# The order of the matmuls within a 128-row chunk of the weight-stationary products

## The chip, the cores and the metric

The kernel runs on one core of one Trainium2 chip. The metric is the device time of one execution in microseconds (us); the median over repeated runs counts. Inputs and outputs are float32 in device memory.

## What is computed

One layer of a decoder trunk on 256 tokens of width 2048, then a final norm. Cut to what matters:

```
h = rms_norm(x);  z = h @ w_in                                  # 2048 x 5144
x = x + concat[gating(z), dilated_attention(z), nsa(z)] @ w_out   # 2048 x 2048
h = rms_norm(x);  m = rms_norm(mem)
x = x + cross_attention(h @ wq, m @ wkv) @ wo
h = rms_norm(x)
x = x + square(relu(h @ w_up)) @ w_down                         # 2048 x 8192, 8192 x 2048
return rms_norm(x)
```

Nearly all of the arithmetic is in the products with weight matrices, and most of that in `w_up` and `w_down`.

## The kernel before

**Products in three parts.** A float32 operand is split into two float32r parts, hi and lo = x - hi. A product sums hi\*hi + hi\*lo + lo\*hi in PSUM. For weights, `split_w` makes `wh` on ScalarE (line 82) and then `wl` on VectorE (line 83) from a loaded block `raw` of 128 x 1024 numbers; `wh` and `wl` have three buffers each, `raw` five. For activations the hi and lo parts of a 128-feature chunk lie side by side, so that one matmul can stream both: 256 tokens of hi, then 256 tokens of lo, 512 columns.

**Two ways round.** `gemm` (line 193) holds activations stationary and streams 512 columns of weights; `w_down` goes that way (tile `dn`, line 207, three matmuls of 512 columns for a chunk). `gemm_t` (line 174) holds weights stationary and streams activations. It makes 256 output features at a time, as two halves f = 0 and f = 1 of 128; each half has one PSUM bank of 512 columns in the tile `acc`, and `acc` has two buffers. `w_up` (tile `up`), `w_out` (`wo`), the queries (`cq`, `bq`, `xq`), keys (`k`, `bk`, `mk`), the gating input (`u`) and the inputs of the compressed branch (`cmp`, issued by a loop of its own at line 259) go that way.

**The function at issue.** `products_t` (line 154) adds one weight block, four chunks kk of 128 rows, to an `acc`. For each chunk and each half it issues two matmuls:

- the **main** one (line 161): 128 weight columns of `wh`, 512 columns of activations (hi and lo), into the whole bank;
- the **low** one (line 165): 128 weight columns of `wl`, 256 columns of activations (hi alone), into the first half of the same bank.

Each matmul has a weight load of its own (LDWEIGHTS, listed as engine PEld). The order within a chunk is low f0, main f0, low f1, main f1, so 256- and 512-column matmuls alternate. Only in the first chunk of an `acc` does main come ahead of low in each half, since the first matmul into a bank must write all of it. After 16 chunks (64 matmuls) `join` (line 185) reads the bank with ScalarE and VectorE.

**The order of the program.** The text of the kernel is not the order on an engine: a scheduler places the instructions of all engines by its own model of their costs, so matmuls of neighbouring tiles can be mixed, and the lists under "The change" show what it made of each version. Weight blocks arrive by DMA issued from SyncE's queue.

**How many.** `products_t` issues 1024 pairs of main and low for `up` (4 quarters of 8 tiles of 32 pairs), 256 for `wo`, 128 for `cq`, and 64 each for `cmp`, `k`, `bk`, `bq`, `u`, `mk` and `xq`: 1856 in all.

Of the kernel before, what the change touches and what calls it, by code (L numbers as in the profile page):

```python
# [13 lines left out]
PSUM = bass.MemoryType.PSUM  # L14

P = 128
S = 256
# [13 lines left out]
# column blocks of w_in that come out transposed, two 128-wide features a pair  # L31
CMP, UU, KV, CQ, BK, BQ = 0, 2, 4, 6, 10, 12
# the parts that a product in float32r takes: hi*hi, hi*lo, lo*hi
# [4 lines left out]
def trunk_kernel(ctx: ExitStack, tc: tile.TileContext, a, out):  # L38
    """Every product with a weight matrix takes its float32 operands as two float32r parts, hi and
    lo = x - hi (exact), and sums hi*hi + hi*lo + lo*hi in PSUM.  # L40

    Activations that feed a product lie transposed, [features, part, tokens], both parts side by side.
    A product comes out transposed (weights stationary, in two halves: hi*hi + lo*hi and hi*lo) or
    with tokens on partitions (activations stationary)."""
    nc = tc.nc
# [12 lines left out]
    ones = cp.tile([P, P], F32, name="ones")  # L58
    nc.vector.memset(ones, 1.0)
    # brings the activation table in before the first data  # L60
# [13 lines left out]
    loads = []  # L74
# [10 lines left out]
    def split_scaled(hi, lo, src, g):  # L85
        """hi + lo = src * g, with g one number a partition."""
        nc.scalar.activation(hi, src, AF.Copy, scale=g)
        nc.vector.scalar_tensor_tensor(lo, src, g, f32(hi), op0=ALU.mult, op1=ALU.subtract)

    def put_act(tiles, k0, src, gi):  # L90
        """src [P, n, S], features k0 .. k0 + n, times their gains."""
        for i in range(src.shape[1]):
            k = k0 + i
            t = tiles[k // 4]
            split_scaled(t[:, k % 4, 0, :], t[:, k % 4, 1, :], src[:, i, :], gT[:, gi, k:k + 1])

# [1 line left out]
    def add_squares(ssq, src, first, eng=None):  # L98
        """ssq [P, 2, S] += src ** 2."""
        sq = ssq if first else sp.tile([P, 2, S], F32, tag="sq", name="sq")  # L100
        if eng is None:
            nc.scalar.activation(sq, src, AF.Square)  # L102
        else:
            eng.tensor_tensor(sq, src, src, op=ALU.mult)
        if not first:
            nc.gpsimd.tensor_tensor(ssq, ssq, sq, op=ALU.add)  # L106

    def mean_eps(ssq, name):
        """mean over features of the squares, + eps: [P tokens, 2]."""
        s = cp.tile([P, 2], F32, name=name)  # L110
        ps = pmisc.tile([P, 2], F32, tag="sc", name="pss")
        nc.gpsimd.tensor_tensor(ssq[:, 0, :], ssq[:, 0, :], ssq[:, 1, :], op=ALU.add)
        for t in range(2):
            nc.tensor.matmul(ps[:, t:t + 1], ssq[:, 0, t * P:(t + 1) * P], ones[:, 0:1], start=True, stop=True)
        nc.vector.tensor_scalar(s, ps, 1.0 / D, EPS, op0=ALU.mult, op1=ALU.add)
        return s
# [6 lines left out]
    def along_free(r, name):  # L123
        """r [P tokens, 2] as [P, S], the same on every partition."""
        b = cp.tile([P, S], F32, name=name)
        ps = pmisc.tile([P, S], F32, tag="sc", name="psb")
        for t in range(2):
            dg = sp.tile([P, P], F32, tag="dg", name="dg")
            nc.vector.tensor_scalar_mul(dg, ident, r[:, t:t + 1])
            nc.tensor.matmul(ps[:, t * P:(t + 1) * P], ones, dg, start=True, stop=True)  # L130
        nc.scalar.activation(b, ps, AF.Copy)
        return b

# [8 lines left out]
    def gemm_t1(x, wsrc, name):  # L142
        """Like gemm_t for a contraction of 512, with one sum: [P, 2 features, tokens]."""
        acc = pacc.tile([P, 2, 2, S], F32, tag="acc", name=name)
        wh, wl = (w.rearrange("p (k n) -> p k n", k=4) for w in split_w(load_raw(wsrc)))
        for kk in range(4):
            for f in range(2):
                fs = slice(f * P, (f + 1) * P)
                for j, (w, l) in enumerate(((wh, 0), (wh, 1), (wl, 0))):
                    nc.tensor.matmul(acc[:, f, 0, :], w[:, kk, fs], x[:, kk, l, :],  # L150
                                     start=(kk == 0 and j == 0), stop=(kk == 3 and j == 2))
        return acc

    def products_t(acc, x, wh, wl, first, last):
        """acc [P, 2 features, hi*hi + lo*hi | hi*lo, tokens] += four 128-row chunks of the contraction."""
        for kk in range(4):
            for f in range(2):
                fs = slice(f * P, (f + 1) * P)

                def main(start, stop):  # L160
                    nc.tensor.matmul(acc[:, f].rearrange("p a s -> p (a s)"), wh[:, kk, fs],  # L161
                                     x[:, kk].rearrange("p a s -> p (a s)"), start=start, stop=stop)

                def low():
                    nc.tensor.matmul(acc[:, f, 0, :], wl[:, kk, fs], x[:, kk, 0, :], start=False, stop=False)  # L165

                if first and kk == 0:
                    main(True, False)
                    low()
                else:  # L170
                    low()
                    main(False, last and kk == 3)

    def gemm_t(lhs, wsrc, name, order=None, between=None):
        """Two 128-wide features, transposed: [P, 2 features, hi*hi + lo*hi | hi*lo, tokens]."""
        acc = pacc.tile([P, 2, 2, S], F32, tag="acc", name=name)
        order = order or list(range(len(lhs)))
        for n, b in enumerate(order):
            wh, wl = (w.rearrange("p (k n) -> p k n", k=4) for w in split_w(load_raw(wsrc[b])))
            products_t(acc, lhs[b], wh, wl, n == 0, n == len(order) - 1)  # L180
            if between is not None:
                next(between, None)
        return acc

    def join(acc, name, dst=None):
        """The two halves of gemm_t, added."""
        lo = sp.tile([P, 2, S], F32, tag="half", bufs=3, name="half")
        nc.scalar.activation(lo, acc[:, :, 1, :], AF.Copy)  # L188
        d = lo if dst is None else dst
        nc.vector.tensor_tensor(d, acc[:, :, 0, :], lo, op=ALU.add)  # L190
        return d

    def gemm(lhs, wsrc, kb, n, name, between=None, hold=0):
        """Tokens on partitions: [P, 2, n]; blocks of kb 128-row chunks of the contraction. The last
        hold blocks stay, and the first tokens go through all of them before the others."""
# [67 lines left out]
    def consts(them):  # L263
        """Not ahead of the weights asked for so far."""
# [16 lines left out]
    # nothing is scaled before the norm is there  # L281
# [24 lines left out]
    # lo, hi and none: one product with hi and one with lo sum what is needed in two halves  # L306
# [6 lines left out]
    def compress():  # L313
        for m, which in enumerate(("k", "v")):
# [7 lines left out]
            # rows 0..29: hi*hi + hi*lo, rows 30..59: lo*hi  # L322
# [26 lines left out]
            else:  # L349
                # v_c of a group at the partitions 32 h of each of its heads  # L350
# [24 lines left out]
    # no compressed block lies before the first rows  # L375
# [8 lines left out]
    def softmax_pair(sc0, sc1, m0, m1, name):  # L384
        """Masked scores of two heads (or branches), both token tiles: exp(s - max) and its sums."""
# [15 lines left out]
    def scale_and_transpose(v0, v1, r, name):  # L401
        """p * r, transposed: [keys, 2, 384], the first 256 columns of keys 0..127, then 128 of the rest."""
# [20 lines left out]
    mix = [None] * 4  # L423
    for g in range(2):
# [5 lines left out]
        # compressed branch, four heads at once  # L430
# [135 lines left out]
    # w_out: the spatial gating's features last; the memory's loads among the products  # L566
# [76 lines left out]
    for q in range(4):  # L643
# [16 lines left out]
        for n in range(4):  # L660
# [3 lines left out]
            for t in range(2):  # L664
# [7 lines left out]
                if q == 3 and n == 2:  # L672
                    # what the last quarter adds comes to this
# [43 lines left out]
def _blocks(w, kb, n):  # L717
    """[K, N] -> [N / n, K / (128 kb), 128, kb * n]: what one partition reads is contiguous."""
    k = w.shape[0]
# [3 lines left out]
def _arrays(np, i):  # L723
# [15 lines left out]
    # cmp, u, selected k, window k, NSA q, dilated k, dilated q  # L739
# [43 lines left out]
```

## Time and profile before

| | |
|---|---|
| median of 3 runs | 1216.53 us (1216.46 to 1218.69) |
| profiled execution, from its first to its last instruction | 1216.0 us |
| TensorE matmuls (PE) busy | 1187.0 us, 98% |
| TensorE weight loads (PEld) busy | 1021.3 us, 84% |
| VectorE (DVE) busy | 750.9 us, 62% |
| ScalarE (ACT) busy | 588.3 us, 48% |
| DMA, mean over the span | 184 GB/s |
| granted TensorE clock, mean | 0.993 |

The profile lists no separate device time for the profiled execution; its span stands 0.5 us under the median of the runs. An engine's busy time is the union of its instructions' spans. Matmuls overlap: the next one starts before the one ahead of it has left the array, so what a matmul costs is the distance between the starts of two matmuls, not its listed length. The listed ends of matmuls are modelled; the starts are recorded.

### The profile page before, as it was taken

What the parts mean: (1) busy time and instruction counts of PE and PEld (TensorE: products, weight loads), DVE (VectorE), ACT (ScalarE), POOL (GpSimd) and SP (SyncE); (2) the same over time, 40 slices, a digit from 0 to 9 for tenths busy, and PEclk for the clock granted to TensorE, in tenths of its full rate; (3) what the DMA queues carried; (4) which work ended last, traced back from release to release, by engine and by line L of the source; (5) the groups of instructions that cost most, each with busy time, mean ns of one, the idle gap of its engine ahead of it and who ended that gap; (6) DMA issues with size and microseconds to landing.
All of it is one profiled execution on the core that took longest, in us unless ns stands there. A gap on an engine that the chain in (4) does not pass through costs nothing.

```text
span 1216.0 us, 16456 instructions
## 1 busy us (share of the span) xinstructions
PE 1187.0 (98%) x6450; PEld 1021.3 (84%) x6450; DVE 750.9 (62%) x904; ACT 588.3 (48%) x800; POOL 61.3 (5%) x54
## 2 busy tenths in 40 slices
PE   5999999999999999999999999999999999999996
PEld 4899888888878888988888888888888888888885
DVE  8775788467687565865554556554565555566554
ACT  5464555365565455644433444433444433444443
POOL 7000000000033100200000000000000000000000
PEclk9999999999999999999999999999999999999999
DMA  6676533555657555555666655666556566655663
GB/s 228 196 252 209 157 122 122 182 158 172 190 191 224 176 172 174 181 177 192 189 195 191 191 186 182 192 201 193 187 178 192 191 196 195 186 185 185 195 189 104
DMA packets 65385, 224.24 MB, mean 184 GB/s; under 512 B 7963, under 2 KB 9499, under 8 KB 65179
## 3 DMA queue, kind: packets, MB, share of 16 engines
q1 hardware_dynamic: 65307, 223.19, 57.8%
q8 instruction: 50, 0.82, 0.3%
q14 instruction: 28, 0.23, 0.1%
HBM read 221.06 MB, written 2.10 MB: 184 GB/s over the span
## 4 chain that ended last, share of the span: by engine, by line
PE 91%; DVE 4%; issue 2%; ACT 1%; DMA 1%; SPq 0%; ACTq 0%; POOLq 0%; POOL 0%; DVEq 0%
PE dn L207 27%; PE up L161 20%; PE up L165 10%; PE wo L161 3%; PE cq L161 2%; DVE wl L83 2%; PE xo L150 2%; PE bv L207 2%; PE v L207 2%; PE mv L207 2%; PE wo L165 2%; PE cq L165 1%; PE xq L161 1%; PE mk L161 1%; PE u L161 1%
## 5 line engine op out<-in xcount | busy, mean ns | idle before, releaser
L83 DVE TENSOR_TENSOR wl<-raw,wh 128x1024 fp32r<-128x1024 f32 (+3 forms) x414 | 505.2, 1224 | 350.5 <-ACT wh L82 348.8
L82 ACT ACTIVATE wh<-raw 128x1024 fp32r<-128x1024 f32 (+3 forms) x414 | 428.8, 1038 | 459.9 <-PE dn L207 185.5
L161 PE MATMUL up<-h,wh 128*128 128x512 f32 x1024 | 359.3, 398 | 0.0
L207 PE MATMUL dn<-wh,hid 128*128 128x512 f32 x992 | 306.2, 389 | 0.0
L165 PE MATMUL up<-h,wl 128*128 128x256 f32 x1024 | 282.4, 281 | 0.0
L161 PEld LDWEIGHTS up<-h,wh 128*128 128x128 f32 x1024 | 190.6, 188 | 44.1
L207 PEld LDWEIGHTS dn<-wh,hid 128*128 128x128 f32 x992 | 186.2, 188 | 38.4
L165 PEld LDWEIGHTS up<-h,wl 128*128 128x128 f32 x1024 | 193.3, 189 | 2.7
L207 PE MATMUL dn<-wl,hid 128*128 128x512 f32 x496 | 193.1, 389 | 0.6 <-DVE sf L675 0.6
L207 PEld LDWEIGHTS dn<-wl,hid 128*128 128x128 f32 x496 | 93.1, 188 | 20.5 <-DVE wl L83 1.0
L161 PE MATMUL wo<-mix,wh 128*128 128x512 f32 x256 | 89.5, 395 | 0.4 <-ACT wh L82 0.4
L165 PE MATMUL wo<-mix,wl 128*128 128x256 f32 x256 | 70.7, 282 | 3.3 <-DVE wl L83 3.3
L161 PEld LDWEIGHTS wo<-mix,wh 128*128 128x128 f32 x256 | 47.5, 188 | 10.9 <-ACT wh L82 0.7
L165 PEld LDWEIGHTS wo<-mix,wl 128*128 128x128 f32 x256 | 48.3, 189 | 5.2 <-DVE wl L83 4.5
L188 ACT ACTIVATE half<-up 128x512 f32<-128x512 f32 x32 | 19.1, 597 | 56.7 <-PE up L161 56.7
L161 PE MATMUL cq<-hx,wh 128*128 128x512 f32 x128 | 45.5, 397 | 0.0
L190 DVE TENSOR_TENSOR half<-up,half 128x512 f32<-128x512 f32 x32 | 22.1, 692 | 35.5 <-ACT half L188 35.5
L106 POOL TENSOR_TENSOR ssq<-ssq,sq 128x512 f32<-128x512 f32 x21 | 30.6, 1456 | 174.6 <-ACT sq L102 174.2
L680 POOL TENSOR_TENSOR rf<-sf,mhalf 128x1 f32<-128x1 f32 x2 | 1.1, 560 | 706.8 <-DVE sf L678 706.8
L165 PE MATMUL cq<-hx,wl 128*128 128x256 f32 x128 | 35.3, 281 | 0.0
L161 PE MATMUL cmp<-hx,wh 128*128 128x512 f32 x64 | 27.6, 463 | 4.6 <-ACT wh L82 4.6
L666 DVE SCALAR_TENSOR_TENSOR xt<-dn,m,xt 128x512 f32<-128x512 f32 x32 | 22.6, 747 | 14.3 <-PE dn L207 14.3
(282 smaller groups left out, 1409.9 us busy)
## 6 DMA issues: line engine op xcount, KB each, us to landing
raw<-in_w_up SPq DMA_DIRECT2D x128, 512.0 KB, 4.3
raw<-in_w_down SPq DMA_DIRECT2D x128, 512.0 KB, 4.3
raw<-in_w_t SPq DMA_DIRECT2D x52, 512.0 KB, 3.6
raw<-in_w_out SPq DMA_DIRECT2D x32, 512.0 KB, 4.3
raw<-in_w_bv SPq DMA_DIRECT2D x8, 512.0 KB, 3.7
raw<-in_w_v SPq DMA_DIRECT2D x8, 512.0 KB, 3.5
raw<-in_w_mk SPq DMA_DIRECT2D x8, 512.0 KB, 4.2
raw<-in_w_q SPq DMA_DIRECT2D x8, 512.0 KB, 3.8
```

What stands on the lines that cost most here:

```text
L82: nc.scalar.activation(hi, src, AF.Copy)
L83: nc.vector.tensor_tensor(lo, src, f32(hi), op=ALU.subtract)
L106: nc.gpsimd.tensor_tensor(ssq, ssq, sq, op=ALU.add)
L150: nc.tensor.matmul(acc[:, f, 0, :], w[:, kk, fs], x[:, kk, l, :], start=(kk == 0 and j == 0), stop=(kk == 3 and j == 2))
L161: nc.tensor.matmul(acc[:, f].rearrange("p a s -> p (a s)"), wh[:, kk, fs], x[:, kk].rearrange("p a s -> p (a s)"), start=start, stop=stop)
L165: nc.tensor.matmul(acc[:, f, 0, :], wl[:, kk, fs], x[:, kk, 0, :], start=False, stop=False)
L188: nc.scalar.activation(lo, acc[:, :, 1, :], AF.Copy)
L190: nc.vector.tensor_tensor(d, acc[:, :, 0, :], lo, op=ALU.add)
L207: nc.tensor.matmul(acc[t][:, :n], lhs[k // 4][:, k % 4, l, ts], w[:, kk, :], start=(k == 0 and j == 0), stop=(k == KD - 1 and j == 2))
L666: nc.vector.scalar_tensor_tensor(xs, acc[t], r3[:, t:t + 1], xs, op0=ALU.mult, op1=ALU.add)
L680: nc.gpsimd.tensor_tensor(rf, s_, mhalf[:, 0:1], op=ALU.pow)
```

## The change

`products_t` issues a chunk's matmuls by kind rather than by half: both mains, then both lows. In the last chunk of an `acc` both lows come first, then both mains, so that the main still closes each bank. Nothing is added or removed; comments and docstrings fall away, and lines after the function move by two (line 165 becomes 166).

```diff
         for kk in range(4):
-            for f in range(2):
-                fs = slice(f * P, (f + 1) * P)
-
-                def main(start, stop):
-                    nc.tensor.matmul(acc[:, f].rearrange("p a s -> p (a s)"), wh[:, kk, fs],
-                                     x[:, kk].rearrange("p a s -> p (a s)"), start=start, stop=stop)
-
-                def low():
-                    nc.tensor.matmul(acc[:, f, 0, :], wl[:, kk, fs], x[:, kk, 0, :], start=False, stop=False)
-
-                if first and kk == 0:
-                    main(True, False)
-                    low()
-                else:
-                    low()
-                    main(False, last and kk == 3)
+            xk = x[:, kk].rearrange("p a s -> p (a s)")
+
+            def mains(start, stop):
+                for f in range(2):
+                    nc.tensor.matmul(acc[:, f].rearrange("p a s -> p (a s)"), wh[:, kk, f * P:(f + 1) * P], xk,
+                                     start=start, stop=stop)
+
+            def lows():
+                for f in range(2):
+                    nc.tensor.matmul(acc[:, f, 0, :], wl[:, kk, f * P:(f + 1) * P], x[:, kk, 0, :],
+                                     start=False, stop=False)
+
+            if last and kk == 3:
+                lows()
+                mains(False, True)
+            else:
+                mains(first and kk == 0, False)
+                lows()
```

**In the MLP's first product.** TensorE's list where one `up` tile ends and the next begins, before (the number behind a tile's name is a buffer's):

```order
L161 MATMUL up_8865<-h_4433,wh 128x512
L165 MATMUL up_8865<-h_4433,wl 128x256
L161 MATMUL up_8865<-h_4433,wh 128x512
L161 MATMUL up_8960<-h_4430,wh 128x512
L165 MATMUL up_8960<-h_4430,wl 128x256
L161 MATMUL up_8960<-h_4430,wh 128x512
L165 MATMUL up_8960<-h_4430,wl 128x256 x2
L161 MATMUL up_8960<-h_4430,wh 128x512
L165 MATMUL up_8960<-h_4430,wl 128x256
L161 MATMUL up_8960<-h_4430,wh 128x512
```

And the same place now:

```order
L166 MATMUL up_4862<-h_4433,wl 128x256 x2
L161 MATMUL up_4862<-h_4433,wh 128x512 x2
L166 MATMUL up_4862<-h_4433,wl 128x256 x4
L161 MATMUL up_4862<-h_4433,wh 128x512 x2
L161 MATMUL up_4963<-h_4430,wh 128x512 x2
L166 MATMUL up_4963<-h_4430,wl 128x256 x2
L161 MATMUL up_4963<-h_4430,wh 128x512 x2
L166 MATMUL up_4963<-h_4430,wl 128x256 x2
```

Before, two mains stood next to each other only where the tile changed, and two lows only where the new tile's first chunk ends; now they stand in twos throughout, and four lows and four mains meet at the tile's end.

**Where the program starts.** TensorE's list where the `cmp` products go over to the second block of x (`hx_81`), before:

```order
L165 MATMUL cmp_85<-hx_80,wl 128x256
L161 MATMUL cmp_85<-hx_80,wh 128x512
L165 MATMUL cmp_84<-hx_81,wl 128x256
L161 MATMUL cmp_84<-hx_81,wh 128x512
L165 MATMUL cmp_84<-hx_81,wl 128x256
```

And now:

```order
L161 MATMUL cmp_85<-hx_80,wh 128x512 x2
L166 MATMUL cmp_85<-hx_80,wl 128x256 x2
L161 MATMUL cmp_84<-hx_81,wh 128x512 x2
L166 MATMUL cmp_84<-hx_81,wl 128x256 x2
L161 MATMUL cmp_84<-hx_81,wh 128x512 x2
```

The first matmul of a new block was one that needs `wl`; it is now one that needs `wh`, and two mains stand ahead of the first that needs `wl`.

## Rows read from the trace of the kernel before

**Rows 1.** The page: span, and busy time, share and instructions of two engines

```profile
span 1216.0 us, 16456 instructions
...
PE 1187.0 (98%) x6450; PEld 1021.3 (84%) x6450; DVE 750.9 (62%) x904; ACT 588.3 (48%) x800; POOL 61.3 (5%) x54
```

**Rows 2.** Waits of PE: total us, times, longest us

```profile
PE cmp L165 <- DVE wl L83: 9.7, 4, 3.9
...
PE wo L165 <- DVE wl L83: 3.3, 3, 1.7
```

**Rows 3.** Chain that ended last, in order of time: start us, us, what

```profile
93.77 8.16 PE wv L207 x68
...
587.04 87.04 PE dn L207 x384
...
764.37 87.04 PE dn L207 x384
...
941.70 87.04 PE dn L207 x384
...
1119.04 57.13 PE dn L207 x252
```

**Rows 4.** Timeline of PE over a tile's end: start us, us, instruction, count

```profile
700.00 0.28 PE L165 MATMUL up<-h,wl 128*128 128x256 f32 x1
...
707.18 0.40 PE L161 MATMUL up<-h,wh 128*128 128x512 f32 x1
707.42 0.28 PE L165 MATMUL up<-h,wl 128*128 128x256 f32 x1
707.54 0.62 PE L161 MATMUL up<-h,wh 128*128 128x512 f32 x2
708.00 0.28 PE L165 MATMUL up<-h,wl 128*128 128x256 f32 x1
708.11 0.40 PE L161 MATMUL up<-h,wh 128*128 128x512 f32 x1
708.35 0.40 PE L165 MATMUL up<-h,wl 128*128 128x256 f32 x2
708.58 0.40 PE L161 MATMUL up<-h,wh 128*128 128x512 f32 x1
708.82 0.28 PE L165 MATMUL up<-h,wl 128*128 128x256 f32 x1
```

**Rows 5.** Timeline of PEld, the weight loads, in the same stretch

```profile
707.06 0.19 PEld L161 LDWEIGHTS up<-h,wh 128*128 128x128 f32 x1
707.18 0.19 PEld L165 LDWEIGHTS up<-h,wl 128*128 128x128 f32 x1
```

**Rows 6.** Timeline of PE in the same alternation in `wo`

```profile
371.03 0.39 PE L161 MATMUL wo<-mix,wh 128*128 128x512 f32 x1
...
374.50 0.39 PE L161 MATMUL wo<-mix,wh 128*128 128x512 f32 x1
```

**Rows 7.** The page: costliest groups, of the mains of `up`

```profile
L161 PE MATMUL up<-h,wh 128*128 128x512 f32 x1024 | 359.3, 398 | 0.0
```

**Rows 8.** Timeline of PE: the longest wait in `cmp`, the last in `wo`

```profile
30.43 0.58 PE L165 MATMUL cmp<-hx,wl 128*128 128x256 f32 x1 [3.92 <-DVE wl L83]
...
366.98 0.39 PE L165 MATMUL wo<-mix,wl 128*128 128x256 f32 x1 [1.75 <-DVE wl L83]
```

**Rows 9.** Stretches: us, then PE, PEld, DVE, ACT, POOL busy, PEclk, DMA share, GB/s

```profile
20.00:30.00 10.00, 4.62 (x16) 3.67 (x16) 10.00 (x8) 3.60 (x6) 9.06 (x7) 0.78 0.45 123
30.00:36.00 6.00, 5.57 (x18) 4.80 (x19) 4.24 (x7) 0.04 (x1) 0.00 (x0) 0.51 0.64 193
...
320.00:370.00 50.00, 46.34 (x260) 39.35 (x259) 41.13 (x49) 30.67 (x49) 12.94 (x9) 1.00 0.60 195
```

## The prediction

> **What bounds the kernel now.** Read the busy shares first: PE has 98% of the span, no other engine over 62% [rows 1]. So what counts is the spacing of matmuls, and the few places where PE waits. Read the waits next: the large ones are 9.7 us in `cmp` and 3.3 us in `wo`, all of lows (line 165) for `wl`, the last thing that VectorE makes of a block [rows 2]. Everywhere else the time is the sum of distances from one matmul's start to the next.
>
> The chain of work gives clean distances. In `dn` 384 matmuls of 512 columns take 87.04 us, 0.2267 us each; in `wv` 68 of 256 columns take 8.16 us, 0.1200 us each [rows 3]. A main and a low by themselves would thus cost 0.3467 us. In `up`, where they alternate, 21 pairs go from a low's start at 700.00 to one at 707.42: 0.3533 us a pair [rows 4]. Whole stages say the same: `dn` ends at 587.04 + 87.04 = 674.08 and begins again at 764.37, so the 256 pairs of a quarter of `up` took 90.29 us, 0.3527 us each (the next quarters 90.29 and 90.30) [rows 3]. So alternation costs 0.006 us a pair over the two kinds by themselves, 6.1 us over `up`'s 1024 pairs [rows 7]. That is what this change can move.
>
> Where the 0.006 us sits is seen in the weight loads. The load for a matmul starts when the matmul ahead of it starts: the load for a low starts at 707.18, with the main [rows 4, 5]. A load is listed with 0.19 us. Under a main (0.23 us) it is done in time; under a low (0.12 us) it isn't, and the main that follows is stretched: a main behind a low takes 0.24 us (707.18 to 707.42), while two mains together take 0.46 (707.54 to 708.00), so that one of them takes 0.22 to 0.23 [rows 4].
>
> **The change part by part.** *Dense stretches.* Every chunk becomes main, main, low, low; the lists show it everywhere but at tile ends, where four of a kind meet. One stretched main in a chunk instead of two. The trace of before holds both pieces: main, main 0.46 us; low, low 0.23 us (708.35 to 708.58) [rows 4]. Starts are rounded to 0.01, so a chunk is 0.69 to 0.70 us, where alternation has 2 x 0.3527 = 0.7054. I take 0.70, the upper end, since these pieces stood singly among alternating ones: 0.0054 us saved on a chunk, times 512 chunks of `up`, 2.8 us. The lower bound of a chunk is 2 x 0.3467 = 0.6934, all of the excess gone: 512 x 0.012 = 6.1 us.
>
> *The other products.* Leaving `cmp` aside there are 768 pairs, 384 chunks. Their alternation isn't always dear: in `wo` ten pairs go from 371.03 to 374.50, 0.347 us each, with no excess at all [rows 6]. So alternation has a dear and a free rhythm, and these stages have both. I take half of `up`'s saving: 0.0027 us. Of the chunks I leave out the 55 or so between 326 and 367 us (41 us less 3.3 of waits, at 0.70 each), where VectorE's 41.13 us of 50 [rows 9] and the wait at 366.98 [rows 8] say that `wl` sets the pace: 329 x 0.0027 = 0.9 us. Bounds: nothing, to 329 x 0.0066 (from 0.70 to the floor of 0.6934) = 2.2 us; below nothing where the free rhythm is lost (the third rival).
>
> *Waits for wl.* A block now begins with two mains, which need `wh` but not `wl`. Where PE waits for `wl`, 0.46 us of work moves ahead of the wait. In `cmp` the last wait is 3.92 us long and ends at 30.43 [rows 8]; VectorE was busy for all of the ten us before [rows 9], so PE's pace doesn't set when `wl` comes, and the three waits ahead of it give nothing that lasts. I count one such gain, 0.46 us, and another for the last wait in `wo`. Together 0.9 us; the bounds are zero (if hi and lo of the activations aren't there either) and 0.46 for each of the seven waits in these two [rows 2], 3.2 us. After the wait at 30.43 the granted clock is 0.51, the lower level of 1.2 GHz, in the stretch to 36 us [rows 9]: PE had been idle for 3.92 us before. With 0.46 us of work put in front of it the idle time is still some 3.5 us; I leave that stretch as it is.
>
> *What is not changed.* The matmuls, loads, DMAs and their order on SyncE's and GpSimd's queues are the same. On ScalarE and VectorE a few instructions of the attention stages change places; PE is not waiting there, and I price that at zero, within 1 us either way. `wh` is released by the second main and `wl` by the last low, 0.23 us apart at most, and no split was waited for in `up`. No wait is added: at a tile's end the mains still close both banks, and the next tile has the other buffer of `acc`.
>
> Sum: 2.8 + 0.9 + 0.9 = 4.6 us off a span of 1216.0, so 1211.4. The median of the runs lies 0.5 us over the span: **1211.9 us**.
>
> A rule to weigh against this. The measured distances depend on the neighbour: 0.24 us for a main behind a low against 0.2267 in a run of mains [rows 3, 4]. The Trainium skill, TensorE: Matmul & The Clock Gate, section Back-to-back issue gap, gives a matmul of N columns N/2.4 + 2.5 ns on its own, which knows no neighbour: 0.216 and 0.109 us here, the same sum in any order, no change from the dense stretches. The trace doesn't agree with its size (0.2267 and 0.1200) nor with its independence.
>
> **The rivals.**
>
> *No change in the dense stretches.* The 0.006 us may belong to each load that lies under a low, not to each main behind a low. In both orders half of the loads lie under lows, so a chunk would stay at 0.7054 and the second low would pay what the second main saves. For it: a low lasts 0.12 us, less than a load's listed 0.19. Against: in `wv` every load lies under a 256-column matmul and the spacing is a clean 0.1200 [rows 3]; low, low in `up` took 0.23 [rows 4]. Only the waits remain: 1216.5 - 0.9 = 1215.6 us.
>
> *All of the excess goes.* The stretch is a rhythm that a run of equal matmuls ends (`dn`, `wv`, and the free rhythm in `wo`). Then 6.1 + 2.2 + 0.9 = 9.2 us: 1207.3 us. Against: the pieces in [rows 4] still show 0.24 for a main behind two lows (708.58 to 708.82).
>
> *Slower.* Two lows in a row have two loads under them, one after the other, and the delay of the second adds to that of the first; both mains then are stretched to 0.24 and 0.235, as mains behind a low are now, and the lows keep their 0.118 each: 0.711 a chunk. That is 0.0056 us over alternation, on the same 512 + 329 chunks 4.7 us, less 0.9 for the waits: 1216.5 + 3.8 = 1220.3 us. It decides from the point at which a chunk costs over 0.7065 us, where the waits no longer pay for it. For it: the main behind two lows is no shorter than the one behind a single low. Against: the second main of [rows 4] is.
>
> That the change doesn't do what it says is ruled out by the lists: mains stand in twos throughout.
>
> **How the numbers follow.** A measurement of this kernel can tell about 0.2%, 2.4 us, from no change. Forecast (1209.5 to 1214.1): 0.55. No change: 0.21. All of it: 0.12. Slower: 0.12. Faster by over 0.2% takes the forecast and the full gain, 0.67, less a little that falls short: 0.66. Within 0.2% 0.22, slower 0.12. The range leaves out most of the slower case and the lower part of the full gain: 1207.0 to 1217.5.
>
> **What would show it.** In the chain, `up`'s quarter goes from 90.29 to about 89.6 us (128 chunks of 0.70); 88.8 is the full gain, 90.3 none, 91.0 the slower rival. In the timeline, main, main should read 0.46 and low, low 0.23 to 0.24 all along, with the second main at 0.22 to 0.23. The waits for `wl` in `cmp` and `wo` should each be some 0.4 us shorter. Quarters that stay at 90.3 make the prediction wrong; so does a second low that takes 0.13 us or more.

## The result and the profile after

The changed kernel takes 1211.3 us (median of 4 runs, 1208.45 to 1211.99) against 1217.23 us in the same comparison: ratio 0.9938, 95% interval 0.9923 to 0.9954, so 5.6 to 9.4 us less. It was forecast at 1211.9 us, with 4.6 us off the span; the span of the profiled execution fell by 6.8 us, from 1216.0 [rows 1] to 1209.2. That execution's own time was 1211.03 us, so 1.8 us lie around the span, not the 0.5 us that the prediction took from the median: two errors that partly cancel in the forecast time. The 0.5 us set the span of one execution against the median of others; every execution on record that lists both has 1.7 to 1.9 us around its span, those of the kernel before too.

The page of the changed kernel, its span and busy engines:

```profile
span 1209.2 us, 16465 instructions
...
PE 1184.4 (98%) x6450; PEld 1018.7 (84%) x6450; DVE 752.0 (62%) x904; ACT 585.7 (48%) x800; POOL 63.5 (5%) x54
```

TensorE is the bound as before [rows 1]. Its waits (total us, times, longest) answer to [rows 2]:

```profile
PE cmp L166 <- DVE wl L83: 7.9, 6, 4.0
PE cmp L161 <- ACT wh L82: 5.0, 3, 4.4
...
PE wo L166 <- DVE wl L83: 0.6, 1, 0.6
```

The waits for `wl` in `wo` have nearly gone, 0.6 us for 3.3; in `cmp` they are 7.9 for 9.7. The longest wait in `cmp` has neither become shorter nor ended earlier than in [rows 8], where it ended at 30.43 us:

```profile
30.45 0.80 PE L166 MATMUL cmp<-hx,wl 128*128 128x256 f32 x2 [4.04 <-DVE wl L83]
```

The chain that ended last, which answers to [rows 3]:

```profile
582.45 87.05 PE dn L209 x384
...
758.81 87.05 PE dn L209 x384
...
935.18 87.05 PE dn L209 x384
...
1111.54 57.15 PE dn L209 x252
```

A quarter of `up`, from the end of `dn` to its next start, is 758.81 - 582.45 - 87.05 = 89.31 us, then 89.32 and 89.31; it was 90.29. `dn` is as it was. The timeline of TensorE in `up` answers to [rows 4] (x2 stands for two in a row):

```profile
703.28 0.40 PE L166 MATMUL up<-h,wl 128*128 128x256 f32 x2
703.51 0.63 PE L161 MATMUL up<-h,wh 128*128 128x512 f32 x2
703.98 0.40 PE L166 MATMUL up<-h,wl 128*128 128x256 f32 x2
704.22 0.63 PE L161 MATMUL up<-h,wh 128*128 128x512 f32 x2
704.68 0.40 PE L166 MATMUL up<-h,wl 128*128 128x256 f32 x2
704.91 0.63 PE L161 MATMUL up<-h,wh 128*128 128x512 f32 x2
705.38 0.39 PE L166 MATMUL up<-h,wl 128*128 128x256 f32 x2
```

Two lows take 0.23 to 0.24 us and two mains 0.46 to 0.47; from 703.28 to 705.38 three chunks take 2.10 us, 0.70 each.

Where the 6.8 us went, by the first matmul of each stage in the two traces:

| stretch | before, us | after, us | difference |
|---|---|---|---|
| start to the first matmul of `k` (`cmp`) | 44.49 | 44.07 | -0.42 |
| `k` to `u` (attention, gating) | 253.32 | 252.97 | -0.35 |
| `wo` | 95.15 | 91.37 | -3.78 |
| `mk` to `xo` (cross attention) | 102.13 | 102.51 | +0.38 |
| `up`, first quarter | 91.79 | 91.36 | -0.43 |
| `up`, other three | 270.88 | 267.95 | -2.93 |
| `dn`, first three quarters | 261.12 | 261.15 | +0.03 |
| last `dn` and the tail | 97.16 | 97.86 | +0.70 |

So `up` gave 3.4 us, a little more than the 2.8 forecast, and `wo` 3.8, far more than the 1 us or less expected there. The tail gave 0.7 us back: the chain there goes through waits for splits and for DMA. This is not the price of arriving earlier, since groups of eight (below) arrive there earlier still and take 97.17 us for it, the 97.16 of before.

### The profile page after: what moved, and what is told of

It reads as the page before. It is cut to its first block, busy times and chain, and to the rows that moved or that the text cites. A ratio compares the mean times of both kernels' runs of the same rounds, so it can differ in the third digit from the quotient of the medians.

```text
span 1209.2 us, 16465 instructions
## 1 busy us (share of the span) xinstructions
PE 1184.4 (98%) x6450; PEld 1018.7 (84%) x6450; DVE 752.0 (62%) x904; ACT 585.7 (48%) x800; POOL 63.5 (5%) x54
## 4 chain that ended last, share of the span: by engine, by line
PE 91%; DVE 2%; DMA 2%; ACT 1%; issue 1%; ACTq 0%; POOLq 0%; POOL 0%; DVEq 0%
PE dn L209 27%; PE up L161 20%; PE up L166 10%; PE wo L161 4%; PE cq L161 2%; PE xo L150 2%; PE wo L166 2%; PE v L209 2%; PE bv L209 2%; PE mv L209 2%; PE k L161 1%; PE mk L161 1%; PE cq L166 1%; PE bq L161 1%; PE xq L161 1%; PE u L161 1%
## 5 line engine op out<-in xcount | busy, mean ns | idle before, releaser
L161 PE MATMUL up<-h,wh 128*128 128x512 f32 x1024 | 317.2, 395 | 0.0
L166 PEld LDWEIGHTS up<-h,wl 128*128 128x128 f32 x1024 | 187.6, 188 | 42.2
L166 PE MATMUL up<-h,wl 128*128 128x256 f32 x1024 | 197.0, 279 | 0.0
L161 PEld LDWEIGHTS up<-h,wh 128*128 128x128 f32 x1024 | 158.3, 189 | 2.6
L161 PE MATMUL wo<-mix,wh 128*128 128x512 f32 x256 | 79.6, 396 | 0.1
L166 PE MATMUL wo<-mix,wl 128*128 128x256 f32 x256 | 49.7, 280 | 0.6 <-DVE wl L83 0.6
L161 PE MATMUL cq<-hx,wh 128*128 128x512 f32 x128 | 40.4, 396 | 0.0
L161 PEld LDWEIGHTS wo<-mix,wh 128*128 128x128 f32 x256 | 39.4, 189 | 1.1 <-ACT wh L82 0.5
L161 PE MATMUL cmp<-hx,wh 128*128 128x512 f32 x64 | 24.1, 478 | 5.1 <-ACT wh L82 5.0
L82 ACT ACTIVATE hid<-half 128x512 fp32r<-128x512 f32 x32 | 20.3, 633 | 17.2 <-DVE half L650 17.2
```

Source lines behind the costliest of these rows:

```text
L82: nc.scalar.activation(hi, src, AF.Copy)
L166: nc.tensor.matmul(acc[:, f, 0, :], wl[:, kk, f * P:(f + 1) * P], x[:, kk, 0, :], start=False, stop=False)
```

## The experiments

Two questions were open. What makes the dense stretches cheaper: the room that a weight load has (the prediction's reason), or something else? And what took the waits out of `wo`: the mains ahead of `wl`, or the new order of VectorE's instructions that the scheduler made along with the change? The quarter of `up` is read in every run from the same two rows of the chain: start and length of one `dn` quarter, and start of the next. The floor for a quarter is 256 x (0.2267 + 0.1200) = 88.75 us, from the runs of one length in [rows 3].

**Twos, lows first.** The dense change without a main ahead of `wl`:

```diff
-            if last and kk == 3:
-                lows()
-                mains(False, True)
-            else:
-                mains(first and kk == 0, False)
-                lows()
+            if first and kk == 0:
+                mains(True, False)
+                lows()
+            else:
+                lows()
+                mains(False, last and kk == 3)
```

> Twos as in the changed kernel, but lows ahead of mains (only the first chunk of an acc keeps main first, without regrouping it: both mains, then both lows). TensorE gets no main ahead of the wait for wl, and VectorE's list in the w_out stage is that of the kernel before. Theory (the dense gain comes from twos, and the large gain in the w_out stage came with VectorE's new order, not with the twos): a quarter of up takes 89.3 us as in the changed kernel (90.3 before); the wait of wo for wl stays near the 3.3 us of before; total about 3.5 to 4 us under before. Rival (mains ahead of wl removed the waits of wo): the same numbers, so this run alone does not tell them apart; the next one does. Rival (the order main, main, low, low matters, not twos): the quarter stays at 90.3.

Median 1215.09 us against 1217.46, ratio 0.9974 (0.9963 to 0.9985). Its chain, and its waits in `wo`:

```profile
587.07 87.05 PE dn L209 x384
...
763.44 87.05 PE dn L209 x384
```

```profile
PE wo L166 <- DVE wl L83: 3.1, 3, 2.0
```

A quarter is 763.44 - 587.07 - 87.05 = 89.32 us: all of the dense gain is there, whichever kind comes first. The waits of `wo` are those of before, and its stage took 96.27 us. So twos alone are worth 3.3 us in `up`, but the total fell by only some 2.4 to 2.7 us, less than the 3.5 to 4 expected, since `wo` was 1.1 us longer than before. The trace shows why: after the longest of these waits the granted clock fell. TensorE's timeline there, and the stretch from 366 to 370 us in the form of [rows 9]:

```profile
365.98 0.51 PE L166 MATMUL wo<-mix,wl 128*128 128x256 f32 x2 [2.00 <-DVE wl L83]
366.32 1.03 PE L161 MATMUL wo<-mix,wh 128*128 128x512 f32 x2
...
369.97 1.09 PE L161 MATMUL wo<-mix,wh 128*128 128x512 f32 x4
```

```profile
366.00:370.00 4.00, 4.00 (x15) 3.43 (x16) 2.20 (x2) 0.00 (x0) 0.00 (x0) 0.57 0.72 215
```

TensorE had waited 2.00 us; then the granted clock was 0.57 over four us, for most of them the lower level of 1.2 GHz, and three chunks took 369.97 - 366.32 = 3.65 us instead of 3 x 0.70 = 2.1. That is about 1.5 us, more than the 1.1 us by which `wo` grew. In the kernel before, behind the wait of 1.75 us at this place, the granted clock stayed at 1.00:

```profile
367.00:371.00 4.00, 4.00 (x23) 3.54 (x24) 3.10 (x4) 0.94 (x1) 0.00 (x0) 1.00 0.74 194
```

**Alternating, main first.** One main ahead of `wl`, no twos:

```diff
-                if first and kk == 0:
-                    main(True, False)
-                    low()
-                else:
-                    low()
-                    main(False, last and kk == 3)
+                if last and kk == 3:
+                    low()
+                    main(False, True)
+                else:
+                    main(first and kk == 0, False)
+                    low()
```

> Alternation as before, but main ahead of low in every half, so one main stands ahead of the first matmul that needs wl; VectorE's order around the last wait of wo is that of before. Theory (twos make the dense gain): a quarter of up stays at 90.3 us. For the waits: if a main ahead of wl shortens each wait by a main's 0.23 us and no more, wo's wait for wl falls from 3.3 us by at most 3 x 0.23 to about 2.6; if mains ahead of wl were the cause of the 2.7 us that the changed kernel gained there, it falls to 1 us or less. Rival (it is enough that the main comes first in its half): the quarter falls to 89.3.

Median 1217.34 us, ratio 0.9997 (0.9988 to 1.0006): no change.

```profile
586.11 87.06 PE dn L207 x384
...
763.57 87.06 PE dn L207 x384
```

```profile
PE wo L165 <- DVE wl L83: 3.1, 3, 1.7
```

A quarter is 90.40 us, not shorter than before. The waits of `wo` are 3.1 us: a main ahead of `wl` didn't give the 0.23 us a wait that theory allowed. The stage was 94.39 us for 95.15.

**VectorE's order alone.** In the changed kernel the scheduler cut the split of the last memory block (`mT`, four instructions of VectorE) in two, with a weight block's `wl` between. VectorE's timeline before, and in the changed kernel:

```profile
362.05 3.74 DVE L88 SCALAR_TENSOR_TENSOR mT<-raw,gT,mT 128x256 fp32r<-128x256 f32 x4
365.71 2.35 DVE L83 TENSOR_TENSOR wl<-raw,wh 128x1024 fp32r<-128x1024 f32 x2
```

```profile
360.01 1.92 DVE L88 SCALAR_TENSOR_TENSOR mT<-raw,gT,mT 128x256 fp32r<-128x256 f32 x2
361.84 1.21 DVE L83 TENSOR_TENSOR wl<-raw,wh 128x1024 fp32r<-128x1024 f32 x1
362.98 1.91 DVE L88 SCALAR_TENSOR_TENSOR mT<-raw,gT,mT 128x256 fp32r<-128x256 f32 x2
```

Before, `wl` stood behind 3.74 us of `mT`, and TensorE waited 1.75 us for it at 366.98 [rows 8]. The experiment keeps the matmul order of before and puts the second half of that split behind the next weight block's (in its trace it came to stand behind the `wl` of two blocks, not of one):

```diff
-            for kk in range(4):
+            for kk in range(2 if j == 3 else 4):
                 split_scaled(mT[j][:, kk, 0, :], mT[j][:, kk, 1, :], raw[:, kk, :], gT[:, 2, 4 * j + kk:4 * j + kk + 1])
...
+        if n == 6:
+            for kk in range(2, 4):
+                with tc.issue_after(splits[at].ins):
+                    nc.scalar.activation(mT[3][:, kk, 0, :], late[:, kk, :], AF.Copy, scale=gT[:, 2, 12 + kk:13 + kk])
+                with tc.issue_after(splits[at].ins):
+                    nc.vector.scalar_tensor_tensor(mT[3][:, kk, 1, :], late[:, kk, :], gT[:, 2, 12 + kk:13 + kk],
+                                                   f32(mT[3][:, kk, 0, :]), op0=ALU.mult, op1=ALU.subtract)
```

> The matmul order of before everywhere. Only the last memory block's split in the w_out stage is cut in two, and the second half (two ScalarE, two VectorE instructions) is put behind the next weight block's split, as the scheduler happened to do in the changed kernel. Theory (VectorE's new order took wo's last wait away, not the matmul order): the wait at 367 us (1.75 us before) goes to under 0.3, wo's waits for wl fall from 3.3 to about 1.6 us, the stage from 95.15 to about 93.5 us; quarters of up stay at 90.3. Rival (two mains ahead of wl did it): the wait only moves, to the block behind the second half, and the stage stays at 95.

Median 1216.06 us against 1217.15, ratio 0.9985 (0.9975 to 0.9995).

```profile
PE wo L165 <- DVE wl L83: 1.5, 2, 0.8
```

The wait of 1.75 us is gone, the others stand; the stage took 93.02 us, 2.1 less than before, and a quarter of `up` is unchanged at 90.29. So more than half of the 3.8 us that `wo` gained is a by-product of the scheduler's list for VectorE, which needs no change of the matmul order at all. The total fell by 1.1 us only; in its trace `cmp` ended 0.33 us later than before (`k` starts at 44.82 us). The other 1.7 us that `wo` gained are not isolated: neither twos without a main ahead of `wl` nor one main ahead without twos shortened its waits by more than 0.2 us.

**Longer runs.** If alternation costs something where the kinds change, longer runs should cost less. Groups of eight (all of a block) and of four (condensed: `mains` and `lows` now loop over the G chunks from k0 on):

```diff
-        for kk in range(4):
+        for k0 in range(0, 4, G):          # G = 4: groups of eight; G = 2: groups of four
...
-            if last and kk == 3:
-                lows()
-                mains(False, True)
+            if last and k0 + G == 4:
+                lows(k0)
+                mains(k0, False, True)
             else:
-                mains(first and kk == 0, False)
-                lows()
+                mains(k0, first, False)
+                lows(k0)
```

> All eight mains of a weight block, then its eight lows (in an acc's last block lows first). Theory (the excess sits where lows and mains meet, some 4 to 6 ns at each change from lows to mains, and runs of one kind have none): a quarter of up takes 88.75 us, the floor of 128 x 0.6934, plus 32 changes x 0.006 or less, 88.8 to 89.0; total 1.5 to 3 us under the changed kernel. Rival (each load under a low costs its share, whatever the order): 89.3 or more. Rival (longer runs of lows fall behind because loads take 0.12 us or more each): above 89.3.

> Two chunks at a time: four mains, then four lows. Theory (a price for each change from lows to mains): a quarter of up between the changed kernel's 89.3 and that of groups of 8, some 89.0 us (88.75 plus 64 changes x 0.0044). Rival (only the step from alternation to twos matters, the rest is a fixed cost of the lows): 89.3.

Groups of eight: 1206.01 us, ratio 0.9905 (0.989 to 0.992), the first version that beats the changed kernel. Groups of four: 1212.43 us, 0.9958 (0.9944 to 0.9971). Chains, of eight and then of four:

```profile
579.45 87.07 PE dn L210 x384
...
755.74 87.04 PE dn L210 x384
```

```profile
582.92 87.04 PE dn L210 x384
...
759.66 87.04 PE dn L210 x384
```

A quarter is 89.22 us with eights, no better than the 89.31 of twos, and 89.70 us with fours, worse. Both expectations missed. The timeline with eights:

```profile
690.47 1.12 PE L166 MATMUL up<-h,wl 128*128 128x256 f32 x8
691.42 2.00 PE L160 MATMUL up<-h,wh 128*128 128x512 f32 x8
693.26 1.11 PE L166 MATMUL up<-h,wl 128*128 128x256 f32 x8
```

Eight lows take 0.95 us, a little less than 8 x 0.1200; the eight mains behind them 1.84, more than 8 x 0.2267 = 1.81. Where in the eight this sits, the same timeline shows when it is read from 692.80 us on, so that its first row holds the last three of them:

```profile
692.59 0.84 PE L160 MATMUL up<-h,wh 128*128 128x512 f32 x3
```

The first five mains take 692.59 - 691.42 = 1.17 us, for 5 x 0.2267 = 1.13, the last three 0.67, for 0.68. The starts in the trace, read to the ns, give these eight mains 0.233, 0.236, 0.228, 0.233, 0.231 and then 0.226 to 0.227 us, and the lows behind them 0.113, 0.119 and then 0.120. So what a change costs is paid over the five mains behind the lows, 27 ns in all, and 7 to 8 ns of it come back in the lows behind the mains.

The gain of eights over the changed kernel is for the most part not in `up` but where `wl` is waited for: 2.4 of the 3.9 us between the two spans lie in `cmp`, whose waits for `wl` fall from 7.9 us to

```profile
PE cmp L166 <- DVE wl L83: 0.9, 1, 0.9
```

The first matmul of `k`, just behind `cmp`, starts at 44.49 us before and 44.32 with lows first (none ahead), 44.00 with one, 44.07 with two (the change), 42.96 with four, 41.65 with eight. With the order of before it was also seen at 44.82 (the run with the split in two), so only the last two differ clearly.

**Sixteens in up.** Groups of eight, with the second block of each `up` tile turned round:

```diff
-            if last and k0 + 4 == 4:
+            if (last or lows_first) and k0 + 4 == 4:      # lows_first: up, second block
                 lows(k0)
-                mains(k0, False, True)
+                mains(k0, False, last)
```

> Groups of eight, and in up the second block of every acc has its lows first, so that runs of sixteen form and a tile has two changes from lows to mains instead of three. Theory (a price of about 15 to 20 ns a change when runs are long): a quarter of up from 89.23 to about 89.0 to 89.1 us, the total 0.5 to 1 us under groups of eight. Rival (price by matmul, not by change): 89.2.

1204.82 us, ratio 0.9898 (0.9883 to 0.9913); the interval overlaps that of eights.

```profile
579.41 87.04 PE dn L210 x384
...
755.52 87.04 PE dn L210 x384
```

A quarter is 89.07 us, as expected (89.0 to 89.1).

**The width of the lows.** This tells whether the excess is a matter of room for the weight load. Order of before, lows of another width:

```diff
-                    nc.tensor.matmul(acc[:, f, 0, :], wl[:, kk, fs], x[:, kk, 0, :], start=False, stop=False)
+                    nc.tensor.matmul(acc[:, f].rearrange("p a s -> p (a s)")[:, :W], wl[:, kk, fs],
+                                     x[:, kk].rearrange("p a s -> p (a s)")[:, :W], start=False, stop=False)
```

> The order of before, with each low 320 columns wide instead of 256: it also adds the lo*lo part for 64 tokens, and leaves nothing out. A low by itself would cost 0.120 + 64 x 0.000417 = 0.147 us (the slope from 0.1200 at 256 and 0.2267 at 512 columns), a quarter of up 256 x (0.2267 + 0.147) = 95.6 us. Theory (the excess comes from weight loads that do not fit under a low): with more room under the low the excess goes, 95.6 us. Rival (the excess belongs to the change of length itself, whatever the room): 95.6 + 1.5 = 97.1 us.

> The order of before, with each low 192 columns wide: the lo*hi part of 64 of the 256 tokens is left out. By the same slope a low would cost 0.0933 us, a quarter of up 256 x 0.32 = 81.9 us. Theory (loads do not fit under a low, and a load needs about 0.12 us): the low's slot does not shrink, the quarter stays at 88 to 90 us. Rival (the change of length itself): 81.9 + 1.5 = 83.4 us.

And the same widths in groups of eight:

> Groups of eight mains and eight lows, each low 320 columns wide (adds the lo*lo part for 64 tokens). Theory (loads): a run of lows at 0.147 us, and no stretched mains behind them, a quarter of up at 95.6 us; with 256 columns the mains behind eight lows read 0.234, 0.235, 0.229, 0.232 and 0.231. Rival (the change of length): the same stretch of 15 ns at each of 32 changes, 96.1 us.

> Groups of eight, each low 192 columns wide (the lo*hi part of 64 tokens left out). A run of lows shows what a load needs: by columns alone 0.0933 us a low and 81.9 us a quarter; theory (a load needs about 0.12 us): 0.11 to 0.12 a low, and 87 to 89 us a quarter.

Each of these runs, and each of the two with matmuls of one length below, is a single execution; the quarters within one agree to 0.01 us. Chains, in that order:

```profile
616.97 87.06 PE dn L208 x384
...
801.10 87.06 PE dn L208 x384
```

```profile
580.98 87.08 PE dn L208 x384
...
756.04 87.09 PE dn L208 x384
```

```profile
606.04 87.07 PE dn L210 x384
...
789.16 87.04 PE dn L210 x384
```

```profile
572.79 87.07 PE dn L210 x384
...
746.79 87.04 PE dn L210 x384
```

With 320 columns a quarter is 97.07 us alternating and 96.05 in eights; by columns alone it is 95.58. The excess is 1.49 and 0.47 us, what it is with 256 columns (1.54 and 0.47). More room under the low changes nothing: the theory of the loads falls, and the rival's numbers, 97.1 and 96.1, are met. With 192 columns a quarter is 87.98 and 86.93 us, far over the 81.9 by columns alone. The timeline of eight lows of 192 columns shows why:

```profile
694.11 1.03 PE L166 MATMUL up<-h,wl 128*128 128x192 f32 x8
694.98 2.01 PE L160 MATMUL up<-h,wh 128*128 128x512 f32 x8
```

They take 0.87 us, 0.109 each, not 0.093. Here the loads most likely do set the pace; no run takes the loads away, so this is argued and not shown. If so, a load needs about 0.11 us, and under a low of 0.12 us it fits.

**Matmuls of one length.** If the room isn't it, is it the change of length, or the change between `wh` and `wl` or between banks, which happens at the same places? Lows of 512 columns (W = 512 above); and mains cut in two:

```diff
-                    nc.tensor.matmul(acc[:, f].rearrange("p a s -> p (a s)"), wh[:, kk, fs],
-                                     x[:, kk].rearrange("p a s -> p (a s)"), start=start, stop=stop)
+                    for half in range(2):
+                        nc.tensor.matmul(acc[:, f, half, :], wh[:, kk, fs], x[:, kk, half, :],
+                                         start=start and half == 0, stop=stop and half == 1)
```

> The order of before, with each low 512 columns wide (it adds the whole lo*lo part): wh and wl still alternate as stationary weights, the matmuls are all of one length. Theory (the excess belongs to the change of length): none, a quarter of up 512 x 0.2267 = 116.1 us. Rival (it belongs to the change between the two weight tiles or between the banks of the two halves): 116.1 + 1.5 = 117.6 us.

> The order of before, with each main cut into two matmuls of 256 columns that load the same weights: three matmuls of one length where there were two of different lengths. Theory (change of length): no excess, 768 x 0.1200 = 92.2 us a quarter of up, 1.9 us over before. Rival (change of weight tile or bank): 92.2 + 1.5 = 93.7 us.

Chains, of the wide lows and then of the cut mains:

```profile
691.60 87.04 PE dn L208 x384
...
894.69 87.04 PE dn L208 x384
```

```profile
592.38 87.07 PE dn L208 x384
...
771.60 87.07 PE dn L208 x384
```

Quarters of 116.05 us (512 x 0.2267 is 116.1) and 92.15 us (768 x 0.1200 is 92.2): no excess in either, with the weight tiles and banks alternating as before. So the excess belongs to the change between matmuls of different lengths, 512 and 256 or 512 and 320 columns.

Put together, with the number of changes from lows to mains in a quarter:

| runs of | quarter, us | over the floor | changes | per change |
|---|---|---|---|---|
| 1 (before) | 90.29 | 1.54 | 248 | 6 ns |
| 2 (the change) | 89.31 | 0.56 | 120 | 5 ns |
| 4 | 89.70 | 0.95 | 56 | 17 ns |
| 8 | 89.22 | 0.47 | 24 | 20 ns |
| 8 and 16 | 89.07 | 0.32 | 16 | 20 ns |
| 1, lows of 320 | 97.07 | 1.49 | 248 | 6 ns |
| 8, lows of 320 | 96.05 | 0.47 | 24 | 20 ns |

A change costs about 20 ns between long runs and 5 to 6 ns between short ones, which is why fours are worse than twos. The starts in the traces show how: a run of two ends before the stretch over five mains does. In the changed kernel's runs of two both mains of `up` take 0.233 us, 13 ns too long together, and both lows 0.116, 8 ns too short together: 5 ns. In runs of four the mains take 0.235, 0.234, 0.232 and 0.229 and the lows 0.119, 0.119, 0.119 and 0.118, so most of the stretch is paid and little comes back. What in TensorE stretches the mains behind lows stays open; no run here shows it. It stays open too why the alternation of before has a free rhythm at times [rows 6].

## Why the prediction was right, point by point

*What bounds the kernel.* Right: distances between matmul starts in the dense stretches, and waits for `wl` in `cmp` and `wo`.

*The size in the dense stretches.* The chunk was put at 0.70 us from pieces in [rows 4] and measures 89.31 / 128 = 0.698. `up` gave 3.4 us for a forecast of 2.8: 2.93 in three quarters and 0.43 in the first, where other work lies among the matmuls. The other products were put at 0.9 us, with half of `up`'s saving on a chunk. Their stages mix them with waits and other work (the attention stages gave 0.35 us, cross attention took 0.38 back), but the starts in the traces, with waits left out, tell the chunk itself: before it took from 0.695 us in `k` to 0.702 in `u`, now it takes 0.697 to 0.698 in all of them. Over their 384 chunks that is some 0.5 us, an estimate from these means: inside the bounds of nothing to 2.2 us, and below the 0.9. The free rhythm was lost where it was, as the forecast allowed: `k` went from 0.6954 to 0.6980.

*The reason for it.* Wrong. The prediction saw a load of 0.19 us spill over a low of 0.12 us and stretch the main behind it, and so expected one of two mains to stay stretched, 0.24 against 0.22. In the changed kernel two mains read 0.46 to 0.47 together, as forecast, but none of them stays at 0.227: both are stretched, to 0.233 us each, and both lows are short, 0.116. And the runs of 320 columns show that room for the load doesn't matter. A load's listed 0.19 us is not the distance that loads need: that is 0.12 us at most, since loads lie under matmuls 0.1200 us apart without any excess, and about 0.11 if it is the load that spaces the lows of 192 columns. By the Trainium skill, TensorE: Matmul & The Clock Gate, section LDWEIGHTS, a load takes its 128 columns / 1.2 ns, 0.107 us; the eight lows of 192 columns agree, with 0.109. That the chunk came out at 0.698 for 0.70 was not the reason's merit: the number was added up from pieces of the trace and so survived the wrong reason.

*The waits.* In `cmp` the forecast was 0.46 us and the gain 0.42. The mechanism fits: the wait ended where it did before (30.45 for 30.43 us), and what follows it is 0.44 us shorter. The size isn't shown by it, since the order of before gave 44.49 and 44.82 us for the same point, and the sign that was named, a wait 0.4 us shorter, didn't come: 4.04 us for 3.92. In `wo` the step that failed is the one that priced VectorE's rearranged instructions at zero, within 1 us, with the words that PE is not waiting there. They were said of the attention stages, and the split that moved in `wo` was not named: in `wo` PE was waiting for VectorE, and the new list was worth 2.1 us by itself. The 0.46 us for mains ahead of `wl` was not shown in `wo`: one main ahead left the waits at 3.1 us.

*The rivals.* No change in the dense stretches: ruled out by the quarter of 89.31. All of the excess goes: `up` gave 0.98 of the 1.54 us of a quarter. Slower: half of its picture is there, both mains are stretched (0.233 us each, for 0.24 and 0.235), but the lows do not keep their 0.118: at 0.116 they give a part back. That a longer regrouping can cost more is seen in the fours, whose quarter is longer than that of twos. The rule with no neighbour, of the Trainium skill's same page, section Back-to-back issue gap, holds within one length (116.05 and 92.15 us, no excess) at larger sizes than the page's, 0.2267 for 0.216 and 0.1200 for 0.109 us; across a change of length the trace doesn't agree.

*The time.* 1211.9 us forecast, 1211.3 measured, with the span 2.2 us lower than forecast and the time around it 1.3 us higher. That the two agree to 0.6 us is in part luck: `wo` gave 2.1 us by a path that had been put at nothing.

## What to carry to other kernels

Where short and long matmuls alternate in a dense stretch, compare the stage with the sum of what runs of each length cost; the difference is the price of changing, and twos or long runs get part of it back; runs of four got back less than either here. Where an engine is waited for, put the work that needs the earlier operand ahead of the work that needs the later one, as much of it as there is: eight mains ahead of `wl` took 2.8 us out of the start, two took 0.4, which is not clear of the scatter. And when a scheduler orders the program, read every engine's list in the stages that wait: a side effect on VectorE was worth 2.1 us here, beside the 3.4 us of the intended change in `up`. Last, look at the granted clock before a stage that came out longer is put down to the order: one wait of 2.00 us was followed by some 1.5 us lost to the clock.

## What the runs showed of the hardware

- A change of the streamed length costs TensorE time of its own: nothing among equal lengths, 5 to 6 ns a change in `up` in runs of one and two, 17 to 20 ns in runs of four and more, the same with short matmuls of 256 and of 320 columns. It is spread over the five long matmuls behind a run of short ones (0.233, 0.236, 0.228, 0.233, 0.231 us, then 0.227). In some stretches the alternation of before cost nothing [rows 6].
- With a weight load for each, matmuls of one length follow at 0.2267 us (512 columns) and 0.1200 us (256) [rows 3], eight of 192 columns at 0.109 us on average, where more than the columns sets the distance, most likely the load.
- After a wait of TensorE of 2.00 us the granted clock fell to its lower level for some 3 us (0.57 over 366 to 370 us); at the same place of the kernel before, after 1.75 us, it stayed at 1.00. No run tells what made the difference.
